# Layer 0's input projection by seven block products in two phases, and its attention by rows

## The chip, the core and the metric

The kernel runs on one core of one Trainium2 chip. The metric is the time of one execution in microseconds (us). Of its engines, TensorE (PE in the profile) multiplies, VectorE (DVE) and ScalarE (ACT) compute on tiles in SBUF and PSUM, GpSimd (POOL) and SyncE (SP) here mainly start DMA transfers. Each engine runs its instructions in order. PSUM has eight banks that each hold one 128 x 512 tile of results.

## The reference

Two decoder layers act on one sequence of 512 tokens of width 2048: layer 0 is gated linear attention (4 heads, keys of 256, values of 512), layer 1 is latent attention. Around each stands a norm before and one after, and the result is added to the input. The change concerns layer 0, whose core is:

```python
def rms_norm(x, g, eps=NORM_EPS):
    xf = x.astype(jnp.float32)
    y = xf * lax.rsqrt(jnp.mean(xf * xf, axis=-1, keepdims=True) + eps)
    return (y * g.astype(jnp.float32)).astype(x.dtype)
...
    proj = h @ w_in
    q, k, v, gate, gk_low = jnp.split(
        proj, [GLA_QK, 2 * GLA_QK, 2 * GLA_QK + GLA_V, 2 * GLA_QK + 2 * GLA_V], axis=-1)
    gk = gk_low @ w_gk2 + b_gk
    log_a = jax.nn.log_sigmoid(gk.astype(jnp.float32)) / GLA_GATE_TAU
...
    b = jnp.cumsum(log_a, axis=3)
...
    q_e = q * jnp.exp(b)
    k_e = k * jnp.exp(-b)
...
    A = jnp.einsum('bhncd,bhnsd->bhncs', q_e, k_e)
...
    o = rms_norm(o, g_onorm).reshape(B, S, GLA_V)
    return (o * jax.nn.silu(gate)) @ w_out
```

The input projection `h @ w_in` has 6144 columns (q, k 1024 each, v and gate 2048 each) and 16 more of the low-rank gate.

## The kernel before

All float32 products with a long moving side are three passes (`mm3`, lines 123 to 127): each operand is split into a high part and the rest, and high*high, high*low and low*high are summed in PSUM. So a 128 x 128 block against 512 columns is three matmuls. The high parts come from ACT, the low ones from DVE, weights included (`chunk_split`, lines 104 to 121), which loads and splits chunks of 1024 elements a partition through rings of buffers.

`start` (line 224) takes x in four tiles of 128 rows. As each is normed, turned by PE transposes (`xn_t`, line 333) and split into `act_hi` and `act_lo`, its products with the first 256 columns of v follow. `gla` (line 339) then does the other v columns of head 0, the low-rank gate product (`gk_low`, line 378, two passes with weights of 48 columns), the decays of head 0 (`decays`, line 419) and for each head the gate and the q and k columns (`block_t`: weights are stationary, the tokens move, so results come transposed), v (`block_s`), the scores (line 488) and the values (line 529). Values come out as o^T, 4 groups of 128 columns; the sum of squares over a head is a product with a matrix of ones (line 549), and the gate is applied in place. `out_proj` (line 558) takes the gated result straight from SBUF.

The norm's gain of layer 0 is multiplied into the weights as they are split (lines 118 and 119). The order of the instructions on each engine is set by a planner that runs the program through a time model and issues what is ready, within the order of the buffers: a tile's buffer comes free when its last reader is done. No due times are written out, apart from two `issue_after` marks for activation tables.

## Time and profile before

| | us |
|---|---|
| median of 3 runs (lowest, highest) | 1508.31 (1508.22, 1508.54) |
| span of the profiled execution | 1506.9 |
| TensorE busy in it | 1488.6 (99%) |
| VectorE busy | 743.9 (49%) |
| ScalarE busy | 659.8 (44%) |
| GpSimd busy | 35.1 (2%) |
| moved by DMA | 149.96 MB, mean 100 GB/s |

Rows of the profile read: line of the code, engine, operation, result<-inputs, tile size and count, then busy time and the mean of one in ns; in the last column the engine's idle time before it and the work that ended it. A row of the timeline starts with the moment and the duration in us. Matmuls overlap, so what one costs is the distance between two starts, and not its own duration. A row of windows gives the length, the busy times of PE, PE's weight loads, DVE, ACT and POOL with their counts, then the granted clock, the DMA share and the GB/s. A row of the chain of waits has start, length, engine, tile and line.

### The profile page before, as it was taken

Reading aid. Unit: us, or ns where it says so; the run is one execution under the profiler, and the core shown is the slowest. Engines: PE = TensorE matmul, PEld = TensorE weight load, DVE = VectorE, ACT = ScalarE, POOL = GpSimd, SP = SyncE. Lnnn points to the kernel's source line nnn. Section 1 sums busy time; section 2 is a strip of 40 time slices with the busy share of each in tenths; the row PEclk is TensorE's granted clock in tenths of the full one; section 3 lists DMA queues with packets and bytes.
Section 4 is the critical chain, followed back from the end, with each engine's and each line's share of the span. In section 5 each row is a group of like instructions: output and inputs, shape, how many; then the busy total and the mean of one; then the engine's idle time right before and its main releaser. Section 6 shows DMA issues by size and latency. Waiting matters only on the chain.

```text
span 1506.9 us, 20016 instructions
## 1 busy us (share of the span) xinstructions
PE 1488.6 (99%) x7874; PEld 1284.5 (85%) x7874; DVE 743.9 (49%) x1345; ACT 659.8 (44%) x1266; POOL 35.1 (2%) x72
## 2 busy tenths in 40 slices
PE   7999999999999999999999999999999999999998
PEld 6988888888888888888899888888888898888888
DVE  6544653355436445434265443333577767753224
ACT  6542642254225424333254444334566676752222
POOL 2100000000000000100011000000000000000000
PEclk9999999999999999999999999999999999999999
DMA  6423223322331323434253333333222112135222
GB/s 222 122 70 98 71 86 96 101 81 80 89 111 57 98 84 120 132 112 133 98 182 100 92 98 98 97 98 91 78 77 66 49 50 72 66 126 182 97 85 112
DMA packets 117966, 149.96 MB, mean 100 GB/s; under 512 B 17580, under 2 KB 75168, under 8 KB 116464
## 3 DMA queue, kind: packets, MB, share of 16 engines
q1 hardware_dynamic: 114272, 136.86, 29.7%
q0 software_dynamic: 3424, 11.75, 2.4%
q8 instruction: 61, 1.00, 0.3%
q14 instruction: 33, 0.27, 0.1%
q10 hardware_dynamic: 176, 0.07, 0.0%
HBM read 140.08 MB, written 8.59 MB: 99 GB/s over the span
## 4 chain that ended last, share of the span: by engine, by line
PE 97%; DMA 1%; DVE 1%; ACT 0%; issue 0%; SPq 0%; DVEq 0%
PE acc L125 11%; PE acc L126 11%; PE acc L127 11%; PE yo_acc L127 8%; PE yo_acc L125 8%; PE yo_acc L126 8%; PE v_acc L127 5%; PE v_acc L126 5%; PE v_acc L125 5%; PE o_t L127 1%; PE o_t L126 1%; PE q_acc L127 1%; PE q_acc L126 1%; PE q_acc L125 1%; PE o_t L125 1%; PE pt L881 1%
## 5 line engine op out<-in xcount | busy, mean ns | idle before, releaser
L125 PE MATMUL acc<-act_hi,w_hi 128*128 128x512 f32 x768 | 299.6, 390 | 0.0
L126 PE MATMUL acc<-act_hi,w_lo 128*128 128x512 f32 x768 | 299.1, 389 | 0.0
L127 PE MATMUL acc<-act_lo,w_hi 128*128 128x512 f32 x768 | 298.8, 391 | 0.0
L119 DVE SCALAR_TENSOR_TENSOR w_lo<-w_raw,g_in,w_hi 128x512 fp32r<-128x512 f32 (+1 forms) x208 | 139.7, 707 | 206.5 <-ACT w_hi L118 206.4
L118 ACT ACTIVATE w_hi<-w_raw,g_in 128x512 fp32r<-128x512 f32 (+1 forms) x200 | 128.2, 691 | 242.7 <-PE acc L127 166.5
L127 PEld LDWEIGHTS acc<-act_lo,w_hi 128*128 128x128 f32 x768 | 144.2, 188 | 30.6 <-issue 0.7
L125 PEld LDWEIGHTS acc<-act_hi,w_hi 128*128 128x128 f32 x768 | 144.2, 188 | 30.6 <-issue 0.7
L126 PEld LDWEIGHTS acc<-act_hi,w_lo 128*128 128x128 f32 x768 | 144.2, 188 | 29.8
L111 DVE TENSOR_TENSOR w_lo<-w_raw,w_hi 128x1024 fp32r<-128x1024 f32 x64 | 78.4, 1225 | 163.6 <-ACT w_hi L110 163.4
L125 PE MATMUL yo_acc<-w_hi,act_hi 128*128 128x512 f32 (+1 forms) x440 | 153.0, 348 | 0.0
L127 PE MATMUL yo_acc<-w_lo,act_hi 128*128 128x512 f32 (+1 forms) x440 | 152.9, 348 | 0.0
L126 PE MATMUL yo_acc<-w_hi,act_lo 128*128 128x512 f32 (+1 forms) x440 | 152.5, 347 | 0.0
L110 ACT CAST w_hi<-w_raw 128x1024 fp32r<-128x1024 f32 x64 | 67.4, 1053 | 163.1 <-PE yo_acc L126 150.0
L119 DVE SCALAR_TENSOR_TENSOR w_lo<-w_raw,gcol,w_hi 128x512 fp32r<-128x512 f32 (+1 forms) x98 | 64.4, 699 | 106.6 <-ACT w_hi L118 106.4
L126 PE MATMUL v_acc<-w_hi,act_lo 128*128 128x512 f32 (+1 forms) x320 | 112.0, 351 | 0.0
L125 PE MATMUL v_acc<-w_hi,act_hi 128*128 128x512 f32 (+1 forms) x320 | 111.3, 351 | 0.4 <-ACT w_hi L118 0.2
L118 ACT ACTIVATE w_hi<-w_raw,gcol 128x512 fp32r<-128x512 f32 (+1 forms) x98 | 61.3, 677 | 114.6 <-PE acc L127 83.8
L127 PE MATMUL v_acc<-w_lo,act_hi 128*128 128x512 f32 (+1 forms) x320 | 110.5, 349 | 0.0
L125 PEld LDWEIGHTS yo_acc<-w_hi,act_hi 128*128 128x128 f32 x440 | 83.4, 189 | 10.4 <-issue 0.2
L126 PEld LDWEIGHTS yo_acc<-w_hi,act_lo 128*128 128x128 f32 x440 | 83.3, 189 | 10.3
L127 PEld LDWEIGHTS yo_acc<-w_lo,act_hi 128*128 128x128 f32 x440 | 83.2, 189 | 10.4 <-issue 0.2
L126 PE MATMUL yo_acc<-w_hi,y_lo 128*128 128x512 f32 (+1 forms) x200 | 69.5, 348 | 0.0
(300 smaller groups left out, 2724.3 us busy)
## 6 DMA issues: line engine op xcount, KB each, us to landing
w_raw<-in_l_gla_w_in_dram SPq DMA_DIRECT2D x64, 512.0 KB, 3.7
w_raw<-in_l_mla_w_in_dram SPq DMA_DIRECT2D x47, 512.0 KB, 3.7
w_raw<-in_l_gla_w_in_dram SPq DMA_DIRECT2D x64, 256.0 KB, 3.0
w_raw<-in_l_gla_w_out_dram SPq DMA_DIRECT2D x32, 512.0 KB, 3.5
w_raw<-in_l_mla_w_out_dram SPq DMA_DIRECT2D x32, 512.0 KB, 3.5
pw_raw<-in_l_mla_w_kvb_dram SPq DMA_DIRECT2D x64, 128.0 KB, 2.5
xo<-in_x_dram POOLq DMA_DIRECT2D x16, 256.0 KB, 5.7
x1d<-yo SPq DMA_DIRECT2D x4, 1024.0 KB, 6.0
```

Source lines behind the costliest of these rows:

```text
L110: nc.scalar.copy(hi, raw)
L111: nc.vector.tensor_tensor(lo, raw, hi.bitcast(F32), ALU.subtract)
L118: nc.scalar.activation(hi[:, kk, :], raw[:, kk, :], AF.Copy, scale=g)
L119: nc.vector.scalar_tensor_tensor(lo[:, kk, :], raw[:, kk, :], g, hi[:, kk, :].bitcast(F32), ALU.mult, ALU.subtract)
L125: t.matmul(out, lh, rh, start=start, stop=False)
L126: t.matmul(out, ll, rh, start=False, stop=False)
L127: t.matmul(out, lh, rl, start=False, stop=stop)
L881: te.transpose(pt[:, o:o + P], probs[i][:, j * P:(j + 1) * P], self.ident)
```

## The change

The 12 blocks of 512 columns of layer 0's input projection become six pairs: q with k (`qk(0)`, `qk(1)`: two heads each) and v with gate (`vg(0)` to `vg(3)`). For each pair, two halves of the tokens, pairs of row blocks of the weights and the two column blocks form 2 x 2 x 2 blocks, which the Strassen-Winograd form multiplies with seven block products and sums instead of eight. Activations (and sums of them) are now the stationary side throughout; the weights (and sums of them), 512 wide, move.

There are two phases over all six pairs. In the first, `first_four` (line 253 of the changed code) does four of the seven products for each pair into eight PSUM banks `pa0` to `pa7`: for each of the eight pairs of row blocks it loads 512 KB twice, makes three sums on DVE and splits. It writes the partial results `p1` and `vw` to DRAM (`stage`) through POOL's queue. Then `left_rest` (line 374) rebuilds the activation sums in the places they had, and in the second phase `last_three` (line 286) does the other three products into `pb0` to `pb5`, reads the partial results back and forms the four results `c0` to `c3`. For q and k, `qk_evac` (line 579) transposes them in PSUM (`qk_t`), two banks alternating. The decays are made for two heads at once, in 2048-wide operations (line 538), one result for q and one for k.

`start` (line 320) now norms all four row tiles and keeps the turned result in float32 (`ht`), and `left_sums` (line 362) makes sums of the token halves before the first product. The low-rank gate product (`gk_low`, line 498) is 16 matmuls in plain float32 from `ht`, goes to DRAM and is read back by `gk_spread` (line 510) after `left_rest`, since it takes `ht`'s memory. The values (line 657) come by rows of tokens; the norm of a head is per row and ACT's accumulated squares replace the ones product; its gain moves into the output weights. Gated rows go to DRAM (`yd`), and `gla_rows` (line 674) reads them back, transposes and splits them ahead of the output projection.

```diff
@@ build
             self.ln_exp_set()
-            self.start()
             self.gla()
...
+            self.gla_rows()
             self.out_proj(a["l0_gla_w_out"], a["l0_post_norm"],
-                                lambda k: (self.act_hi[:, k, :], self.act_lo[:, k, :]),
-                                self.between, self.cq_ahead)
+                          lambda k: (self.act_hi[:, k, :], self.act_lo[:, k, :]),
+                          self.between, self.cq_ahead, gain=self.gon16)
...
+    def act_slot(self, t, kp, slot, r):
+
+        o = (slot % 2) * 256 + r * P
+        return t[:, 2 * kp + slot // 2, o:o + P]
...
+    def prods(self, ps, kp, slots, hi, lo, ws):
+        for q, (slot, wi) in enumerate(zip(slots, ws)):
+            for r in range(2):
+                self.mm3(ps[2 * q + r], self.act_slot(self.act_hi, kp, slot, r),
+                         self.act_slot(self.act_lo, kp, slot, r), hi[:, wi, :], lo[:, wi, :],
+                         kp == 0, kp == KT // 2 - 1)
+
+    def first_four(self, w, m, n1, n2):
...
+        ps = [self.ps.tile([P, 512], F32, tag="a", name=f"pa{q}", bufs=8) for q in range(8)]
+        for kp in range(KT // 2):
+            r1 = self.raw_pair(w, n1, kp, name="left")
+            r2 = self.raw_pair(w, n2, kp, name="right")
...
+            v.tensor_tensor(t[:, 0, :], r1[:, 0, :], r2[:, 0, :], ALU.add)
+            v.tensor_tensor(t[:, 1, :], t[:, 0, :], r2[:, 1, :], ALU.add)
+            v.tensor_tensor(t[:, 2, :], t[:, 1, :], r1[:, 1, :], ALU.add)
...
+            nc.scalar.copy(hi[:, 1:4, :], t)
+            v.tensor_tensor(lo[:, 1:4, :], t, hi[:, 1:4, :].bitcast(F32), ALU.subtract)
+            self.prods(ps, kp, (0, 2, 1, 3), hi, lo, (0, 2, 1, 3))
+        for r in range(2):
+            p1 = self.stg([P, 512], "p1")
+            nc.scalar.copy(p1, ps[r])
+            nc.gpsimd.dma_start(self.stage[m, :, 0, r, :], p1)
+            u = self.stg([P, 512], "u2")
+            v.tensor_tensor(u, p1, ps[2 + r], ALU.subtract)
+            for i, p in ((1, ps[4 + r]), (2, ps[6 + r])):
+                t = self.stg([P, 512], "vw")
+                v.tensor_tensor(t, u, p, ALU.add)
+                nc.gpsimd.dma_start(self.stage[m, :, i, r, :], t)
...
+    def last_three(self, w, m, n1, n2, evac):
...
+        ps = [self.ps.tile([P, 512], F32, tag="b", name=f"pb{q}", bufs=6) for q in range(6)]
+        done = self.sp.tile([P, 3, 2, 512], F32, tag="done", name="done", bufs=1)
+        nc.gpsimd.dma_start(done, self.stage[m])
+        for kp in range(KT // 2):
...
+            v.tensor_tensor(t, r2[:, 0, :], r2[:, 1, :], ALU.add)
...
+            self.prods(ps, kp, (2, 0, 1), hi, lo, (0, 1, 2))
+        for r in range(2):
+            p2, q3, p7 = ps[r], ps[2 + r], ps[4 + r]
+            c = [self.stg([P, 512], f"c{i}") for i in range(4)]
+            v.tensor_tensor(c[0], p2, done[:, 0, r, :], ALU.add)
+            evac(r, 0, c[0])
...
@@ start
-                self.part_s(s, 4 * i, ws[i], self.v_ps, slice(0, 256), self.act_hi, self.act_lo, KT)
...
+                    v.scalar_tensor_tensor(xt[s][:, c], xt[s][:, c], rstd, gr[:, c], ALU.mult, ALU.mult)
...
+                    nc.scalar.copy(self.ht[:, 4 * g:4 * g + 4, cols], pv)
+                    ks = slice(4 * g + s // 2, 4 * g + 4, 2)
+                    self.split_from(pv[:, s // 2::2, :], self.act_hi[:, ks, cols], self.act_lo[:, ks, cols])
             for g in range(4):
...
+                self.left_sums(xp, g)
...
+    def left_rest(self, g):
...
+        v.tensor_tensor(x[:, :, 0, :], h(1, 1), h(0, 1), ALU.subtract)
+        v.tensor_tensor(x[:, :, 0, :], x[:, :, 0, :], h(0, 0), ALU.add)
+        v.tensor_tensor(x[:, :, 0, :], h(1, 0), x[:, :, 0, :], ALU.subtract)
+        v.tensor_tensor(x[:, :, 1, :], h(0, 0), h(0, 1), ALU.subtract)
...
@@ gla
+        order = [qk(0), vg(0), vg(1), qk(1), vg(2), vg(3)]
...
+                    self.constants()
+                    self.gk_low()
+                    for m, (n1, n2) in enumerate(order):
+                        self.first_four(w, m, n1, n2)
+            with pool("lb", **R) as self.tp:
+                for g in range(4):
+                    self.left_rest(g)
...
+            self.gk_spread()
+            with tc.issue_after(self.ln_exp.ins):
+                self.decays(0)
+            for p in range(2):
+                self.last_three(w, 3 * p, *qk(p), self.qk_evac)
+                for h in (2 * p, 2 * p + 1):
+                    self.scores(h)
+                    self.last_three(w, 3 * p + 1 + h % 2, *vg(h), self.vg_begin(h))
+                    self.values(h)
+                if p == 0:
+                    self.decays(1)
...
@@ gk_low
-            nc.tensor.matmul(ps[0:m, :], wl[:, k, :], self.act_hi[:, k, :], start=k == 0, stop=False)
-            nc.tensor.matmul(ps[0:m, :], wl[:, k, :], self.act_lo[:, k, :], start=False, stop=k == KT - 1)
...
+            nc.tensor.matmul(ps[0:GRANK, :], raw[:, k, :], self.ht[:, k, :], start=k == 0, stop=k == KT - 1)
...
@@ decays, qk_evac
+        nc.scalar.activation(ek, ek, AF.Exp, scale=-1.0)
+        nc.scalar.activation(ek, ek, AF.Ln, bias=1.0)
+        v.tensor_tensor(ek, eq, ek, ALU.subtract)
...
+        pt = self.pt("qk_t")
+        for j in range(4):
+            nc.tensor.transpose(pt[:, j * P:(j + 1) * P], c[:, j * P:(j + 1) * P], self.ident)
...
@@ values, gla_rows
+                self.mm3(po, at(self.at_h, j)[:, c], at(self.at_l, j)[:, c], self.vh[j], self.vl[j],
+                         j == 0, j == i)
...
+            v.scalar_tensor_tensor(y, po, r, y, ALU.mult, ALU.mult)
+            nc.gpsimd.dma_start(self.yd[h, :, i, :], y)
+
+    def gla_rows(self):
...
+            y = self.slot(f"g{h}", [P, ST, GDV], F32, f"y{h}")
+            nc.sync.dma_start(y, self.yd[h])
...
```

Three places in the order of the instructions, before and changed. The first is the start on PE. Before, `v_acc0` are products of v and `xn_t` transposes of normed x:

```order
L333 MATMUL xn_t_125<-cf_87,xn_123 128x128 x4
L333 MATMUL xn_t_134<-cf_87,xn_132 128x128 x4
L125 MATMUL v_acc0_109<-w_hi_159,act_hi_78 128x256
L333 MATMUL xn_t_143<-cf_87,xn_141 128x128 x4
L126 MATMUL v_acc0_109<-w_hi_159,act_lo_79 128x256
L127 MATMUL v_acc0_109<-w_lo_160,act_hi_78 128x256
L125 MATMUL v_acc0_109<-w_hi_159,act_hi_78 128x256
L126 MATMUL v_acc0_109<-w_hi_159,act_lo_79 128x256
```

Now, with `gkl_acc` the low-rank gate product, `gkl_raw` its weights, `ht` the turned x and `pa0` the first product of the new form:

```order
L353 MATMUL xn_t_270<-cf_82,x3_101 128x128 x4
L353 MATMUL xn_t_279<-cf_82,x3_101 128x128 x4
L411 MATMUL gcols_331<-cf_82,rows_323 128x36
L504 MATMUL gkl_acc_367<-ht_75,gkl_raw_365 16x512 x16
L130 MATMUL pa0_388<-w_hi_404,act_hi_66 128x512
L131 MATMUL pa0_388<-w_hi_404,act_lo_67 128x512
L132 MATMUL pa0_388<-w_lo_405,act_hi_66 128x512
```

The products that stood between transposes are gone, and the low-rank gate product stands ahead of the first product of the projection. Its weights come from POOL, whose row waits for the last split of the sums (`act_lo<-lsum_297`) on DVE:

```order
L406 DMA rows_323<-in_l1_pre_norm_dram 16x128
L501 DMA gkl_raw_365<-in_l0_gla_w_in_dram 128x16x16
L445 DMA trigd_361<-sin_cos_353 128x128 x2
L445 DMA trigd_361<-nsn_359 128x128
L508 DMA gkd_386<-gkl_384 16x512
```

On DVE the sums of the token halves (`lsum`) and their splits stand so:

```order
L368 TENSOR_TENSOR lsum_292<-lsum_292,ht_75 128x2x256
L372 TENSOR_TENSOR act_lo_67<-lsum_287,act_hi_66 128x2x512
L372 TENSOR_TENSOR act_lo_67<-lsum_292,act_hi_66 128x2x512
L367 TENSOR_TENSOR lsum_297<-ht_75 128x2x256
L367 TENSOR_TENSOR lsum_302<-ht_75 128x2x256
L368 TENSOR_TENSOR lsum_297<-lsum_297,ht_75 128x2x256
L368 TENSOR_TENSOR lsum_302<-lsum_302,ht_75 128x2x256
L372 TENSOR_TENSOR act_lo_67<-lsum_297,act_hi_66 128x2x512
```

On POOL the load of the weights stands behind the small rows of constants; on DVE four splits and their sums stand behind those of the last row tile.

The second place is the change from the first q/k pair to the first v/gate pair in the second phase, on PE (`pb` are products, `c0` to `c3` results, `qk_t` their transposes):

```order
L132 MATMUL pb2_2902<-w_lo_2947,act_hi_66 128x512
L584 MATMUL qk_t_2788<-cf_82,c0_2783 128x128 x4
L584 MATMUL qk_t_2795<-cf_82,c1_2784 128x128 x4
...
L132 MATMUL pb4_2904<-w_lo_2947,act_hi_66 128x512
L584 MATMUL qk_t_2802<-cf_82,c2_2785 128x128 x4
L584 MATMUL qk_t_2809<-cf_82,c3_2786 128x128 x4
L584 MATMUL qk_t_2820<-cf_82,c0_2815 128x128 x4
L584 MATMUL qk_t_2827<-cf_82,c1_2816 128x128 x4
L130 MATMUL pb5_2905<-w_hi_2914,act_hi_66 128x512
```

and on DVE, where `eq` and `ek` are the decays of two heads:

```order
L551 TENSOR_SCALAR eq_2479<-z_2493,gcol_333 128x512
...
L307 TENSOR_TENSOR c0_2815<-pb1_2520,done_2525 128x512
L309 TENSOR_TENSOR c1_2816<-pb3_2522,done_2525 128x512
L554 TENSOR_TENSOR ek_2480<-eq_2479,ek_2480 128x2048
L556 SCALAR_TENSOR_TENSOR eq_2479<-restart_2476,ek_2480 128x512 x4
L563 TENSOR_TENSOR rest_2505<-eq_2479 128x12
L573 TENSOR_TENSOR ek_2480<-eq_2479 128x2048
...
L588 SCALAR_TENSOR_TENSOR eq_2479<-qk_t_2788,eq_2479 128x4x128
L588 SCALAR_TENSOR_TENSOR eq_2479<-qk_t_2802,eq_2479 128x4x128
L311 TENSOR_TENSOR c2_2817<-pb5_2524,done_2525 128x512
```

Where PE's rows are left out stand 11 products more; `qk_t_2802` takes the bank of `qk_t_2788`, whose reader is the row after the subtraction, the scans and the second subtraction on DVE.

The third place is the entry to the output projection, on SP (`w_raw` are output weights, `y0` to `y3` the gated rows) and on PE (`o_` values, `y_t` transposes):

```order
L103 DMA w_raw_5212<-in_l0_gla_w_out_dram 128x2x512
L103 DMA w_raw_5244<-in_l0_gla_w_out_dram 128x2x512
L103 DMA w_raw_5276<-in_l0_gla_w_out_dram 128x2x512
L679 DMA y0_4944<-yd_69 128x2048
L679 DMA y1_4974<-yd_69 128x2048
L679 DMA y2_5004<-yd_69 128x2048
L679 DMA y3_5034<-yd_69 128x2048
L103 DMA w_raw_5312<-in_l0_gla_w_out_dram 128x2x512
```

On PE:

```order
L130 MATMUL o_4903<-v_hi3_4543,at_h2_4502 128x512
L131 MATMUL o_4903<-v_hi3_4543,at_l2_4505 128x512
L132 MATMUL o_4903<-v_lo3_4547,at_h2_4502 128x512
L683 MATMUL y_t_4946<-cf_82,y0_4944 128x128 x4
L683 MATMUL y_t_4953<-cf_82,y0_4944 128x128 x4
L130 MATMUL yo_acc0_5080<-w_hi_5086,act_hi_66 128x512
```

The load of the gated rows stands behind seven loads of weights, the last of which (`w_raw_5276`) takes a buffer that DVE's split of the fourth (`w_lo_5183`) frees. Before, no such load existed, and products of the output projection stood between those of the last values:

```order
L127 MATMUL yo_acc1_4733<-w_lo_4829,act_hi_78 128x512
L125 MATMUL yo_acc1_4733<-w_hi_4828,act_hi_78 128x512
L126 MATMUL yo_acc1_4733<-w_hi_4828,act_lo_79 128x512
L549 MATMUL o_norm_4675<-o_ssq_4608,ones_547 128x512
L127 MATMUL yo_acc1_4733<-w_lo_4829,act_hi_78 128x512
L125 MATMUL yo_acc2_4734<-w_hi_4828,act_hi_78 128x512
```

More of the change, by code (lines that the diff above doesn't have):

```diff
@@ L44 @@
 SCALE = (NOPE + ROPE) ** -0.5
+NMAC = 6
 GQ0, GK0, GV0, GG0, GL0 = 0, 1024, 2048, 4096, 6144
@@ new lines, in left_sums @@
+    def left_sums(self, pool, g):
+        nc, v = self.nc, self.nc.vector
+        h = lambda odd, half: self.ht[:, 4 * g + odd:4 * g + 4:2, half * 256:(half + 1) * 256]
+        x = pool.tile([P, 2, 2, 256], F32, tag="lsum", name="lsum", bufs=2)
+        v.tensor_tensor(x[:, :, 0, :], h(1, 1), h(0, 1), ALU.subtract)
+        v.tensor_tensor(x[:, :, 1, :], x[:, :, 0, :], h(0, 0), ALU.add)
+        sl = lambda t: (t[:, 4 * g:4 * g + 4, :].rearrange("p (q k) n -> p q (k n)", k=2)[:, :, 256:768]
+                        .rearrange("p q (s n) -> p q s n", s=2))
+        nc.scalar.copy(sl(self.act_hi), x)
+        v.tensor_tensor(sl(self.act_lo), x, sl(self.act_hi).bitcast(F32), ALU.subtract)
@@ L339, in gla @@
     def gla(self):
[L340 removed]
+        nc, tc, a = self.nc, self.tc, self.a
         w = a["l0_gla_w_in"]
[L342 to L363 removed]
@@ L398, in gk_low @@
-        both = self.slot("g3", [96, 1024 + S], FR, "gk2_r")
+        both = self.gp.tile([96, 1024 + S], FR, name="gk2_r")
         self.w2, self.g2 = both[:, 0:1024], both[:, 1024:]
-        for i, t in enumerate(w2):
+        for i in range(2):
+            t = self.tmp([96, 512], F32, f"w2{i}")
             c = slice(i * 512, (i + 1) * 512)
@@ L423, in decays @@
         nc, v = self.nc, self.nc.vector
[L424 to L431 removed]
+        eq = self.bp.tile([P, 4, S], F32, tag="eq", name="eq")
@@ new lines, in decays @@
+            v.tensor_scalar(eq[:, c, :], z, bias, 0.0, ALU.add, ALU.min)
+        nc.scalar.activation(ek, ek, AF.Exp, scale=-1.0)
+        nc.scalar.activation(ek, ek, AF.Ln, bias=1.0)
+        v.tensor_tensor(ek, eq, ek, ALU.subtract)
+        for c in range(4):
+            v.tensor_tensor_scan(eq[:, c, :], self.restart, ek[:, c, :], 0.0, ALU.mult, ALU.add)
+        b = eq.rearrange("p c (j t) -> p (c j) t", t=P)
+        mid = eq.rearrange("p c (j t) -> p c j t", t=P)[:, :, :, GCH - 1]
+        end = eq.rearrange("p c (j t) -> p c j t", t=P)[:, :, :, P - 1]
@@ new lines, in decays @@
+        f = self.st.tile([P, 4, 6], F32, tag="far", name="far", bufs=2)
+        r = self.st.tile([P, 4, 3], F32, tag="rest", name="rest", bufs=2)
+        v.tensor_tensor(r, end[:, :, 0:3], mid[:, :, 0:3], ALU.subtract)
+        for o, i in ((0, 0), (3, 1), (5, 2)):
+            v.tensor_tensor(f[:, :, o:o + 1], r[:, :, i:i + 1], mid[:, :, i + 1:i + 2], ALU.add)
+        v.tensor_tensor(r[:, :, 0:2], r[:, :, 0:2], end[:, :, 1:3], ALU.add)
+        for o, i in ((1, 0), (4, 1)):
+            v.tensor_tensor(f[:, :, o:o + 1], r[:, :, i:i + 1], mid[:, :, i + 2:i + 3], ALU.add)
@@ new lines, in gla_rows @@
+    def gla_rows(self):
+        nc = self.nc
+        for h in range(GH):
+            y = self.slot(f"g{h}", [P, ST, GDV], F32, f"y{h}")
+            nc.sync.dma_start(y, self.yd[h])
+            for s in range(ST):
+                pt = self.pst.tile([P, 512], F32, tag="pt", name="y_t")
+                for j in range(4):
+                    nc.tensor.transpose(pt[:, j * P:(j + 1) * P], y[:, s, j * P:(j + 1) * P], self.ident)
+                cols = slice(s * P, (s + 1) * P)
+                self.split_from(pt.rearrange("p (k n) -> p k n", n=P),
+                                self.act_hi[:, 4 * h:4 * h + 4, cols], self.act_lo[:, 4 * h:4 * h + 4, cols])
@@ L559, in out_proj @@
+    def out_proj(self, w, gpost, y_of, then, ahead=None, gain=None):
         nc, v = self.nc, self.nc.vector
```

363 lines of the change are left out of this document (176 added, 187 removed).

## The prediction

> **What bounds the kernel now.** I read the engine rows of the page first, then the chain of waits, then the spacing of TensorE's instructions.
>
> ```profile
> span 1506.9 us, 20016 instructions
> PE 1488.6 (99%) x7874; PEld 1284.5 (85%) x7874; DVE 743.9 (49%) x1345; ACT 659.8 (44%) x1266; POOL 35.1 (2%) x72
> PE 97%; DMA 1%; DVE 1%; ACT 0%; issue 0%; SPq 0%; DVEq 0%
> ```
>
> TensorE (PE) works without a pause, and the chain that ends last is 97% PE. So the time is the sum of the products' spacings plus the few pauses, and a product that disappears is worth its whole spacing, as long as PE does not wait for what takes its place. The spacing, from the timeline of PE:
>
> ```profile
> 199.66 0.39 PE L127 MATMUL acc<-act_lo,w_hi 128*128 128x512 f32 x1
> 199.88 0.39 PE L125 MATMUL acc<-act_hi,w_hi 128*128 128x512 f32 x1
> ...
> 202.15 0.40 PE L126 MATMUL acc<-act_hi,w_lo 128*128 128x512 f32 x1
> ```
>
> Eleven intervals lie between the first and the last row: (202.15 - 199.66)/11 = 0.2264 us for one 512-wide product. Where layer 0 now hands over to its output projection, and how the first 70 us go:
>
> ```profile
> 599.36 0.58 PE L125 MATMUL yo_acc<-w_hi,act_hi 128*128 128x512 f32 x1
> 0.00:27.00 27.00, 15.96 (x98) 14.54 (x99) 16.99 (x46) 20.44 (x55) 5.24 (x17) 1.00 0.84 283
> 27.00:70.00 43.00, 43.00 (x358) 42.47 (x357) 27.72 (x67) 22.58 (x43) 8.38 (x15) 1.00 0.39 111
> ```
>
> The second and third rows are windows (PE is the first busy time): PE works 16 of the first 27 us and then without a gap, because products of v start on each row tile as it arrives. At 599.4 the first output product starts, with the last score tiles (about 1.3 us), 48 value products of the last head (about 7.5) and one ones product (0.9) still behind it: PE has done all work before the output projection at an equivalent of **609 us**. What follows is alike in both programs: 576 output products of 512 columns, 384 of 256, then layer 1. The gain of the inner norm that moves into the weights' split there (two half-width instructions an engine instead of one) hides under PE's 24 products (5.4 us) a pair of rows. So I forecast only the moment that replaces 609.
>
> **The products.** Before, the six column pairs of the input projection are 12 column blocks x 4 token tiles x 16 rows of blocks x 3 passes = 2304 products; now 6 x 8 x 24 in the first phase and 6 x 8 x 18 in the second, 2016. That is 521.7 us against 456.4: **-65.2 us**. Small work on PE, from these rows:
>
> ```profile
> 202.54 0.86 PE o_norm L549 x2
> 164.27 1.78 PE a_diag L506 x16
> 166.06 1.31 PE a_off L524 x8
> 171.95 1.34 PE a_off L524 x12
> 22.77 0.66 PE L333 MATMUL xn_t<-cf,xn 128*128 128x128 f32 x4 [0.16 <-DVE act_lo L175]
> 23.18 0.36 PE L126 MATMUL v_acc<-w_hi,act_lo 128*128 128x256 f32 x1
> ```
>
> Scores stay 4.43 a head, 17.7 in all. Four 128-wide transposes take 0.41 (22.77 to the next start); 64 new ones for q and k and 64 for the gated rows are 2 x 16 x 0.41 = 13.1. Values by rows are 30 products a head, 4 x 30 x 0.2264 = 27.2; eight z products 1.9. The ones product in plain fp32 (two records) takes 0.86 for 512 columns.
>
> **The start** eats most of the gain. All products of the new form need sums of two row tiles, so none can start until all four tiles are normed, turned and summed. And ahead of them on PE now stands the low-rank gate product, 16 instructions in plain fp32: by the 0.86 row, 13.8 us. It waits for its weights, whose DMA on POOL waits for the last split of the sums (DVE's row act_lo<-lsum, because the memory is only then free).
>
> ```profile
> L330 DVE TENSOR_SCALAR xn<-x,x_rstd x16: 476/482/487, 9.2 to 31.8; 128x512 f32<-128x512 f32 x16
> L111 DVE TENSOR_TENSOR w_lo<-w_raw,w_hi 128x1024 fp32r<-128x1024 f32 x4 | 4.9, 1226 | 5.0 <-ACT w_hi L110 5.0
> L464 DVE SCALAR_TENSOR_TENSOR eqm<-acc,eqm 128x512 f32<-128x512 f32 x8 | 5.5, 684 | 0.0
> L175 DVE TENSOR_TENSOR at_l<-a_off,at_h 128x256 fp32r<-128x256 f32 x3 | 1.3, 425 | 11.9 <-ACT at_h L174 11.9
> gkl_raw<-in_l_gla_w_in_dram POOLq DMA_DIRECT2D x1, 128.0 KB, 4.0
> ```
>
> DVE up to that split, at these durations: 16 norm instructions with two tensors (0.69 each, 11.0), 16 splits of 256 (6.8), 12 weight sums that stand between them (8.3), two weight splits of 512 and two of 1536 (1.4 and, by the slope of 0.54 per 512 from the 512 and 1024 rows, 3.5), 8 sums of act (5.5) and 4 splits of 1024 (4.9): 41 us. DVE began at 9.2 before, so the split ends near 50, or 53 with some waits for ACT. Plus 4.0 for the weights' DMA and 13.8: the first product starts at **71 us** (bounds 64, if DVE keeps the closer pitch of about 0.6 that back-to-back rows show, and 76). Without any stall behind it the handover is at 71 + 456.4 + 13.1 + 1.9 + 17.7 + 27.2 = **587 us**, 22 before today's 609. The change can therefore afford 22 us of stalls.
>
> **The stalls**, each as order of instructions times durations:
>
> ```profile
> L442 DVE TENSOR_TENSOR_SCAN b<-restart,soft 128x512 f32<-128x512 f32 x8 | 9.8, 1222 | 0.2
> L110 ACT CAST w_hi<-w_raw 128x1024 fp32r<-128x1024 f32 x4 | 4.2, 1048 | 4.3 <-PE v_acc L126 4.3
> L438 ACT ACTIVATE soft<-soft 128x512 f32<-128x512 f32 x8 | 5.0, 631 | 0.2
> x1d<-yo SPq DMA_DIRECT2D x4, 1024.0 KB, 6.0
> w_raw<-in_l_gla_w_in_dram SPq DMA_DIRECT2D x64, 512.0 KB, 3.7
> act_hi<-x1d POOLq DMA_DIRECT2D x2, 1024.0 KB, 7.3
> trigd<-sin_cos POOLq DMA_DIRECT2D x2, 64.0 KB, 2.5
> ```
>
> A 2048-wide operation is not in the trace: bounds are the 1024 row and four times the 512 row, and by the slopes I take 2.3 on DVE and 1.9 on ACT.
>
> *Decays.* Late in each q/k column pair PE has given its last z product; then run two ACT operations of 512 (1.3), exp and ln of 2048 (3.8), a DVE subtraction (2.3), four scans (4.9), a second subtraction (2.3), small pieces (1.0) and exp of 2048 (1.9): 17.5 us until DVE empties the first transposed q tile. Two banks hold such tiles, so the third q/k transpose waits for that, and everything of PE stands behind it. In between PE has only 27 products and 8 transposes (6.9): 10.6 idle, and about 1.4 more at the next pair of tiles, 12. In the second q/k pair some 34 products lie between: 10. Together **22** (15 to 30). If the order let PE run on into the next pair's products, this would be nothing; the banks of the next pair are emptied by the same DVE queue.
>
> *Between phases.* After the last product of the first phase, PE can do the 12 products whose act slots stay (2.7), then needs slots rebuilt by DVE sums whose memory is freed when the last partial result has left for DRAM: two DVE results, its DMA on POOL (2.5 to 5), four sums, a cast of 1024, about 13.4 after the last product. Idle **11** (8 to 14).
>
> *Changes of column pair.* PE overtakes the emptying of its banks by one or two DVE results: 1.5 each by the 0.69 row with its cast, five times in the first phase and three in the second: **12** (0 to 20).
>
> *The end.* The gated rows are read back from DRAM. That load stands on SP behind seven loads of output weights, of which the last waits for DVE's split of the fourth; about 26 DVE instructions (16 us) lie between the last product of the input projection and that split, and the load of 1 MB takes 6.0 to 7.3, then transposes and splits 1.2. PE has the 30 value products (6.8) to fill 23.7: idle **16** (10 to 20). If the load stood first it would be covered by nothing but those value products.
>
> Within a phase PE is not overtaken: a pair of row blocks is 24 products, 5.4 us, against 4.5 on DVE (three sums of 0.69, splits of 0.69 and 1.77) and about 2.1 on ACT; in the second phase 4.1 against 2.8 and 1.9. Loads are 1 MB a 5.4 us, two of the 3.7 us rows, on queues whose window row shows 283 GB/s where 193 are needed.
>
> *Clock.* PE pauses longer than any in today's steady part, and its start shows what a cold start does:
>
> ```profile
> 15.75 0.41 PE L125 MATMUL v_acc<-w_hi,act_hi 128*128 128x256 f32 x1
> 15.96 0.41 PE L126 MATMUL v_acc<-w_hi,act_lo 128*128 128x256 f32 x1
> ...
> 18.06 0.28 PE L127 MATMUL v_acc<-w_lo,act_hi 128*128 128x256 f32 x1
> 18.18 0.28 PE L125 MATMUL v_acc<-w_hi,act_hi 128*128 128x256 f32 x1
> ```
>
> The same product is 0.21 apart at 15.8 and 0.12 apart at 18.1, after some 4 us of dense work; the granted clock in the window row reads 1.00 all the same. Four stalls of 9 us or more would each cost 0 to 1.7 us by these rows; I take 3 for all. [...]
>
> **Sum.** 587 + 22 + 11 + 12 + 16 + 3 = 651 against 609: +42. The profiled span of 1506.9 becomes 1549; the median of the runs lies 1.4 above that span, so **1550 us**.
>
> **The rivals.** (A) *Faster, 1497.* The planner's order is better than my walk: scans and sums overlap, DVE keeps 0.6 throughout. With the start at 64, decays 2, phases 5, changes 0 and the end 6, the handover is 580 + 13 = 593, 16 early: 1492; with half of the spared stalls back, 1497. For it: the arithmetic is sure to save 65, and DVE is busy only 49%. Against it: the four waits are on PE in program order, whatever the load. (B) *Some stalls smaller, still slower: 1522.* All at their lower bounds (15, 8, 0, 10) with the start at 71: 587 + 33 = 620, +11, or 1519; 1515 to 1530 when one of them is full. (C) *Slower by much: 1585.* One mechanism, DVE in the first phase: my 4.5 us of a 5.4 pair become 5.9 if DVE runs 30% slower beside the loads; 48 pairs x 0.5 = 24 more, then cold clocks add 4 to 10. For it: three sums and a 1536 split of each pair are new work; against it: the rows of today give DVE one duration from 27 to 70 us, where it is busy 64% of the window (27.72 of 43), and later. (D) *It does not do what it says:* products stay 0.2264 but the stalls eat exactly the gain, 1506 to 1511: it needs 22 us of stalls, less than half of what I walk.
>
> **Chances.** Forecast (1533 to 1570) 0.55; B (1513 to 1533) 0.15; C 0.14; A 0.12; D 0.04. What can be told from no change is about 0.2%, 3 us. The likeliest case's range is 1533 to 1570; for 8 in 10 it reaches down through B and up into C: 1512 to 1582. Faster 0.12, same 0.04, slower 0.84.
>
> **What would show it.** PE busy about 50 to 60 us less, with 95% of the span; first 512-wide product near 71 us behind 16 fp32 products; PE idle of 10 us at two qk_t rows, each released by DVE, with an exp of 2048 in front; idle of about 11 before pb2 of the first second-phase pair; idle of about 16 before y_t, released by a DMA. If the first product starts before 62 us, or if the sum of idle time on PE from there to the output projection is under 22, the forecast is wrong by its sign; if DVE is 90% busy in the first phase, C is it.

## The result, and the profile after

| | before | changed |
|---|---|---|
| median of 4 runs, us | 1508.42 | 1565.57 |
| lowest, highest | 1508.22, 1509.31 | 1561.76, 1567.71 |
| profiled span, us | 1506.9 | 1564.0 |

The ratio is 1.0374 (95%: 1.0359 to 1.0388): the changed kernel is 57 us slower. The forecast was 1550 with a range of 1512 to 1582.

From the page of the changed kernel: the span, the engine rows, the granted clock in 40 slices, and the shares of the chain that ended last.

```profile
span 1564.0 us, 19919 instructions
PE 1463.3 (94%) x7409; PEld 1234.4 (79%) x7409; DVE 978.1 (63%) x1652; ACT 729.7 (47%) x1391; POOL 68.6 (4%) x130
PEclk7799999999899989799999999999999999999999
PE 70%; issue 18%; DVE 6%; DMA 3%; ACT 2%; POOL 1%; SPq 0%; DVEq 0%; POOLq 0%; ACTq 0%
```

PE has 465 instructions fewer. It is busy 25 us less, and the span is 57 us longer. The granted clock, which gave 1.00 over the window from 27 to 70 us before, now falls below nine tenths in five of the slices (slices of 39 us; the first two, the eleventh, the fifteenth and the seventeenth).

Where PE waits, by the work that ended the wait (us in total, times, longest):

```profile
PE xn_t L353 <- DVE x L350: 27.4, 4, 13.0
PE qk_t L584 <- DVE eq L588: 23.2, 4, 11.0
PE gkl_acc L504 <- DMA gkl_raw<-in_l_gla_w_in_dram: 9.5, 1, 9.5
PE pb L130 <- ACT act_hi L384: 7.6, 1, 7.6
PE gcols L411 <- DMA rows<-in_l_pre_norm_dram: 5.2, 1, 5.2
PE o L130 <- DVE sg L671: 4.7, 2, 2.6
PE y_t L683 <- DMA y<-yd: 4.3, 1, 4.3
```

These are the places that the prediction had walked: the start without products (`xn_t` and `gcols`; PE's waits at its start sum to 11 us in the kernel before), the decays, the low-rank gate product, the change of phase, the last values and the reload of the gated rows. The first product of the new form starts here (timeline of PE):

```profile
71.30 1.45 PE L504 MATMUL gkl_acc<-ht,gkl_raw 128*16 128x512 f32 x3
72.68 0.50 PE L130 MATMUL pa<-w_hi,act_hi 128*128 128x512 f32 x1
```

And this is the program by stage (windows: length, busy time of PE, of its weight loads, of DVE, ACT and POOL, then granted clock, DMA share, GB/s): the first phase, the two stalls of the decays, and the end of layer 0's attention.

```profile
72.70:337.00 264.30, 262.88 (x1153) 214.97 (x1152) 215.32 (x261) 101.04 (x108) 17.57 (x33) 1.00 0.68 207
...
398.00:420.00 22.00, 10.50 (x45) 8.52 (x45) 17.46 (x30) 7.16 (x9) 0.55 (x1) 0.69 0.24 85
...
538.00:560.00 22.00, 10.12 (x47) 7.97 (x46) 17.56 (x29) 7.16 (x9) 0.54 (x1) 0.69 0.19 68
...
631.00:656.00 25.00, 12.46 (x33) 8.09 (x31) 17.38 (x29) 16.79 (x39) 3.76 (x7) 0.70 0.57 196
```

The first phase runs as costed: 1152 products at 0.2264 us are 260.8, and it took 264.3. Each stall takes two things. In the 22 us around the decays PE is busy 10.5, and the mean clock of that stretch is 0.69: the work after the stall runs slow too. The first of the two, on PE:

```profile
397.66 0.39 PE L132 MATMUL pb<-w_lo,act_hi 128*128 128x512 f32 x1
408.68 1.09 PE L584 MATMUL qk_t<-cf,c 128*128 128x128 f32 x4 [10.63 <-DVE eq L588]
...
414.37 0.63 PE L132 MATMUL pb<-w_lo,act_hi 128*128 128x512 f32 x1
414.79 0.63 PE L130 MATMUL pb<-w_hi,act_hi 128*128 128x512 f32 x1
```

PE waits 10.63 us for DVE's `eq`, and 6 us after it resumed its products still stand 0.42 apart instead of 0.2264.

### The profile page after: what moved, and what is told of

It is laid out like the page before. It is cut to its first block, busy times and chain, and to the rows that moved or that the text cites. A ratio compares the mean times of both kernels' runs of the same rounds, so it can differ in the third digit from the quotient of the medians.

```text
span 1564.0 us, 19919 instructions
## 1 busy us (share of the span) xinstructions
PE 1463.3 (94%) x7409; PEld 1234.4 (79%) x7409; DVE 978.1 (63%) x1652; ACT 729.7 (47%) x1391; POOL 68.6 (4%) x130
## 4 chain that ended last, share of the span: by engine, by line
PE 70%; issue 18%; DVE 6%; DMA 3%; ACT 2%; POOL 1%; SPq 0%; DVEq 0%; POOLq 0%; ACTq 0%
PE yo_acc L130 8%; PE yo_acc L132 8%; PE yo_acc L131 8%; PE pb L130 4%; PE pb L131 4%; PE pb L132 3%; PE acc L132 3%; PE acc L131 3%; PE acc L130 3%; PE q_acc L132 1%; PE q_acc L131 1%; PE q_acc L130 1%; PE pt L1012 1%; DMA right<-in_l_gla_w_in_dram 1%; PE cq_acc L131 1%
## 5 line engine op out<-in xcount | busy, mean ns | idle before, releaser
L130 PE MATMUL pa<-w_hi,act_hi 128*128 128x512 f32 x384 | 150.4, 392 | 1.4 <-ACT p L274 1.4
L131 PE MATMUL pa<-w_hi,act_lo 128*128 128x512 f32 x384 | 149.5, 389 | 0.0
L130 PE MATMUL pb<-w_hi,act_hi 128*128 128x512 f32 x288 | 116.4, 408 | 12.7 <-ACT act_hi L384 7.6
L132 PE MATMUL pa<-w_lo,act_hi 128*128 128x512 f32 x384 | 118.3, 389 | 0.0
L131 PE MATMUL pb<-w_hi,act_lo 128*128 128x512 f32 x288 | 114.0, 397 | 0.0
L132 PE MATMUL pb<-w_lo,act_hi 128*128 128x512 f32 x288 | 101.0, 398 | 0.8 <-DVE w_lo L302 0.8
L130 PE MATMUL acc<-act_hi,w_hi 128*128 128x512 f32 x256 | 99.7, 389 | 0.0
L131 PE MATMUL acc<-act_hi,w_lo 128*128 128x512 f32 x256 | 99.6, 389 | 0.0
L132 PE MATMUL acc<-act_lo,w_hi 128*128 128x512 f32 x256 | 99.1, 389 | 0.0
L270 DVE TENSOR_TENSOR w_lo<-sums,w_hi 128x1536 fp32r<-128x1536 f32 x48 | 84.2, 1754 | 15.1 <-ACT w_hi L269 15.1
L130 PEld LDWEIGHTS yo_acc<-w_hi,act_hi 128*128 128x128 f32 x440 | 83.7, 190 | 10.5 <-ACT act_hi L179 0.2
```

The lines of the kernel that those rows point to most:

```text
L130: t.matmul(out, lh, rh, start=start, stop=False)
L131: t.matmul(out, ll, rh, start=False, stop=False)
L132: t.matmul(out, lh, rl, start=False, stop=stop)
L270: v.tensor_tensor(lo[:, 1:4, :], t, hi[:, 1:4, :].bitcast(F32), ALU.subtract)
```

## The experiments

The first theory was the prediction's: each stall lies in the order of the instructions, and taking away what makes PE wait gives back the stall. Its rival: a stall that goes comes back a little later as a wait for VectorE, which is busy 63% of the span now. A second question came with the profile: whether the half clock behind a stall is part of the stall's price. All ratios are against the kernel before (1508.44 to 1508.49 in these runs).

**The weights of the low-rank gate early.** They are loaded at the start into a buffer that is there anyway, so that the load waits for no memory.

```diff
@@ start
+        raw = self.wp.tile([P, 2, 512], F32, tag="left2", name="gkl_raw", bufs=3)
+        self.gkl_raw = raw[:, 0, 0:KT * GRANK].rearrange("p (k n) -> p k n", n=GRANK)
+        nc.gpsimd.dma_start(self.gkl_raw, ...)
@@ gk_low
-        raw = self.tp.tile([P, KT, GRANK], F32, tag="gkl_raw", name="gkl_raw")
-        nc.gpsimd.dma_start(raw, ...)
+        raw = self.gkl_raw
```

> One edit: the weights of the low-rank gate product are loaded at the start into a buffer of the weight ring, so that their load no longer waits for the last split of the token-half sums. Theory (the start is a chain: last split, load 4 us, 13.8 us of float32 products in front of the first new product): TensorE's idle of 9.5 us in front of the float32 products goes to under 1 us, the first new product starts at about 63 us instead of 72.7, and the median falls by 9 to 10 us, to about 1556 us. Rival (the start is bound by VectorE, which makes rows, sums and splits): the idle moves from in front of the float32 products to in front of the first new product, which still starts after 70 us, and the median stays at 1562 to 1568 us.

1557.96 us, 1.0334 (1.0318 to 1.035): 7.6 less than the change. The gate product starts at 48.65 instead of 56.8, the first new product at 64.0 instead of 72.68. The wait of 9.5 us for the weights was real, and most of it comes back.

**The gate product behind the first phase.** The other way to have it off the start:

```diff
@@ gla
-                    self.gk_low()
                     for m, (n1, n2) in enumerate(order):
                         self.first_four(w, m, n1, n2)
+                    self.gk_low()
```

> One edit: the low-rank gate product moves from in front of the first phase to behind it, into the place where TensorE waits for the rebuilt activation sums. Theory (at the start the product and the wait for its weights are 18 us of delay; behind the first phase it fills a wait of 11.7 us that is there anyway, and the half clock after that wait comes from its idle time): the first new product starts at 54 to 56 us instead of 72.7, TensorE's idle between the phases falls to 1 to 4 us, no half-clock stretch stands between 320 and 345 us, and the median is 1545 to 1550 us. Rival one (the start is bound by VectorE, which still has weights to split): first new product after 62 us, 1555 us or more. Rival two (the half clock comes from load): the half-clock stretches at the change of phase stay, 1551 to 1556 us.

1549.47, 1.0276 (1.026 to 1.0291): 16.1 less. The first new product starts at 47.3. The gate product now fills the change of phase. Its row in this kernel, and the window of that change here and, in the second fence, in the changed kernel:

```profile
L504 PE MATMUL gkl_acc<-ht,gkl_raw x32: 592/592/603, 320.7 to 334.0; 128*16 128x512 f32 x32
310.00:345.00 35.00, 35.00 (x126) 20.16 (x125) 26.38 (x39) 12.78 (x20) 3.75 (x7) 1.00 0.48 159
```

```profile
310.00:345.00 35.00, 30.90 (x129) 24.57 (x128) 26.16 (x36) 13.53 (x18) 3.23 (x6) 0.94 0.49 158
```

With PE busy through the change of phase the clock stays at 1.00, where it fell in the changed kernel with the same work on the other engines. So here the half clock went with PE's idle time (1.00 against 0.94 in this window). The start gains less than the 25 us by which its first product is earlier: after 21 products PE waits 4.45 us for `gcol`, a copy that stands in DVE's queue behind its work on masks and angles (53.4 to 58.1), and the gate product's own 14 us are only moved.

**The v/gate products ahead of the q/k products.** In each half of the second phase the v/gate products of the first head go ahead of the q/k products, so that PE has 144 products to run while the decays are made.

```diff
@@ gla
             for p in range(2):
+                h = 2 * p
+                self.last_three(w, 3 * p + 1, *vg(h), self.vg_begin(h))
                 self.last_three(w, 3 * p, *qk(p), self.qk_evac)
-                for h in (2 * p, 2 * p + 1):
-                    self.scores(h)
-                    self.last_three(w, 3 * p + 1 + h % 2, *vg(h), self.vg_begin(h))
-                    self.values(h)
+                self.scores(h)
+                self.values(h)
+                self.scores(h + 1)
                 if p == 0:
                     self.decays(1)
+                self.last_three(w, 3 * p + 2, *vg(h + 1), self.vg_begin(h + 1))
+                self.values(h + 1)
```

> One edit: in the second phase the first v/gate pair of each two heads comes before their q/k pair, and the decays of the second two heads are made before the last but one v/gate pair, so that the 17 us chain of exp, ln, scans and exp has a whole pair (about 33 us of products) beside it. Theory (TensorE waits for that chain at the third q/k transpose, and the half clock of 13.65 us after each such stall is set by the idle time itself): both idle stretches of 11 us at qk_t go, with them the half-clock stretches at 402 and 542 us, and the median falls by 23.2 + 6.0 = 29 us, to about 1536 us (1533 to 1542). Rival one (the half clock comes from load, not from idle time): the idle goes but a half-clock stretch stays somewhere between 390 and 560 us, 1540 to 1546 us. Rival two (VectorE is the bound of this part, it is busy 86% from 380 to 420 us): the idle reappears in front of scores or values and the median stays above 1555 us.

1551.70, 1.0288 (1.0271 to 1.0306): 13.9 less, half of what was expected. The waits of PE in this kernel:

```profile
PE o L130 <- DVE at_l L180: 8.6, 2, 7.2
PE pb L130 <- DVE c L307: 7.8, 4, 4.5
...
PE pb L132 <- DVE w_lo L302: 4.6, 3, 3.4
...
PE qk_t L587 <- DVE c L307: 0.4, 1, 0.4
```

The wait of `qk_t` went from 23.2 to 0.4. The first three rows are 21.0 us of waits for DVE. Of these the changed kernel had 1.3 too, and the 8.6 at `at_l` stand at the last values, where it waited 8.3 for other operands. So some 11 us are new, at the results and splits of the next products; the longest split wait, 3.4 us, stands right behind the four scans on DVE. Here the rival holds for half the gain: the decays still occupy DVE, and PE now meets its queue at the next results and splits.

**The decays with less work on ScalarE.** The exp and ln of 2048 columns, 3.8 us of the chain as the prediction had it, are left out, so the decays are not those of the reference.

```diff
@@ decays
-        nc.scalar.activation(ek, ek, AF.Exp, scale=-1.0)
-        nc.scalar.activation(ek, ek, AF.Ln, bias=1.0)
```

> Left out: the exp and the ln of 2048 columns in the decays (two ScalarE instructions of 1.9 us for each two heads), so that the chain between the last z product and the release of the first transposed q tile is 3.8 us shorter. Theory (the stall is that chain less the products beside it): the idle in front of the third q/k transpose falls from 10.6 and 11.0 us to 6.8 and 7.2, and the median falls by 7.6 us of idle and up to 4 us of half clock, to 1554 to 1559 us. Rival (VectorE's queue sets it, whatever ScalarE does): idle stays above 9 us each, 1562 us or more.

1566.28, 1.0385 (1.0369 to 1.04): no gain. DVE's timeline ahead of the stall, first in the changed kernel:

```profile
395.50 2.28 DVE L554 TENSOR_TENSOR ek<-eq,ek 128x2048 f32<-128x2048 f32 x1
397.81 4.57 DVE L556 TENSOR_TENSOR_SCAN eq<-restart,ek 128x512 f32<-128x512 f32 x4
...
402.51 2.28 DVE L573 TENSOR_TENSOR ek<-eq 128x2048 f32<-128x2048 f32 x1
...
407.85 0.69 DVE L588 SCALAR_TENSOR_TENSOR eq<-qk_t,eq 128x512 f32<-128x512 f32 x1 [2.09 <-ACT eq L575]
```

and ScalarE's there:

```profile
390.29 1.92 ACT L552 ACTIVATE ek<-ek 128x2048 f32<-128x2048 f32 x1
392.25 1.91 ACT L553 ACTIVATE ek<-ek 128x2048 f32<-128x2048 f32 x1
405.79 0.22 ACT L571 ACTIVATE far<-far 128x24 f32<-128x24 f32 x1 [11.63 <-DVE far L570]
405.92 1.89 ACT L575 ACTIVATE eq<-ek 128x2048 f32<-128x2048 f32 x1
```

then DVE's without exp and ln:

```profile
394.83 2.28 DVE L552 TENSOR_TENSOR ek<-eq,ek 128x2048 f32<-128x2048 f32 x1
...
397.62 4.56 DVE L554 TENSOR_TENSOR_SCAN eq<-restart,ek 128x512 f32<-128x512 f32 x4
...
407.65 0.69 DVE L586 SCALAR_TENSOR_TENSOR eq<-qk_t,eq 128x512 f32<-128x512 f32 x1 [2.09 <-ACT eq L573]
```

ln ended at 394.16, and the subtraction that takes its result started 1.3 us later, because DVE was in results, sums and splits of the products without a pause. So 3.8 us of ScalarE were worth 0.2 at the end (407.85 to 407.65). The idle time at `qk_t` fell by 2.9 in all (23.2 to 20.3), in part because PE came later to it: it waited 1.15 and 0.56 for results of DVE just ahead. And two other stretches of half clock, those that end the change of phase and the values, came out 3.4 longer each, and the half clock costs 2.8 more in this execution, added up over every product in such a stretch. That leaves no gain, as the rival had it.

**The decays with less work on DVE.** The same question from the other side: the four scans are left out, so the running sums within a chunk are missing.

```diff
@@ decays
-        for c in range(4):
-            v.tensor_tensor_scan(eq[:, c, :], self.restart, ek[:, c, :], 0.0, ALU.mult, ALU.add)
```

> Left out: the four scans (running sums of the log decays) for each two heads, 4.57 us of VectorE in a row. ScalarE's exp and ln of the decays stay. Theory, corrected by the run with shorter decays (there VectorE worked without a pause from 387 to 405.8 us, so its queue and not ScalarE's exp and ln is the chain): the idle in front of the third q/k transpose falls by the whole 4.6 us, from 10.6 and 11.0 to 6.0 and 6.4 us. The median falls by 9 us of idle and up to 7 us more if the half clock gets shorter with it, 1549 to 1557 us. Rival (some other chain of the same length stands beside it, ScalarE or the loads): less than 2 us each, above 1560 us.

1556.47, 1.0318 (1.0301 to 1.0335): 9.1 less. PE's wait (23.2 in the changed kernel), the kernel without exp and ln first, then that without scans:

```profile
PE qk_t L582 <- DVE eq L586: 20.3, 4, 9.7
```

```profile
PE qk_t L582 <- DVE eq L586: 13.0, 4, 5.7
```

Each stall is 5 us shorter than in the changed kernel for 4.57 us of scans. The two runs together put the chain in DVE's queue as far as the second subtraction, and not in the operations in the order in which the data pass through them; behind it DVE does wait, 2.09 us, for ScalarE's exp. No run took out a DVE instruction that stands in this queue and is no part of the decays.

**The gated rows through POOL's queue.** If SP's weight loads ahead hold up the reload, another queue should not.

```diff
@@ gla_rows
-            nc.sync.dma_start(y, self.yd[h])
+            nc.gpsimd.dma_start(y, self.yd[h])
```

> One edit: the gated rows are read back through GpSimd's queue instead of SyncE's, where they stood behind seven loads of output weights. Theory (that place on the queue sets the last wait): TensorE's idle of 4.3 us in front of the first transposes goes, and with it part of the half clock there; the median falls by 4 to 7 us, to 1559 to 1562 us. Rival (the wait is that of the values and the gate on VectorE, and the load would be hidden anyway): the idle grows in front of the value products or stays, 1563 to 1568 us.

1571.05, 1.0408 (1.0392 to 1.0424): 5.5 more. **The rows ahead of the weights.** Here SP's loads of output weights wait until the first load of gated rows is issued, and the rows of the last head, whose writing ends last, go through POOL's queue, so that they hold up nothing on SP.

```diff
+            with tc.issue_after(self.y_load.ins):
                 self.out_proj(...)
@@ gla_rows
-            nc.sync.dma_start(y, self.yd[h])
+            ld = (nc.gpsimd if h == GH - 1 else nc.sync).dma_start(y, self.yd[h])
+            if h == 0:
+                self.y_load = ld
```

> One edit: on SyncE's queue the loads of the gated rows of heads 0 to 2 stand ahead of the loads of output weights instead of behind seven of them; the rows of head 3 are loaded by GpSimd's queue behind their last write. Theory (the place on the queue keeps the load of the first rows 15 us behind the last projection product): the load starts near 631 us instead of 646, TensorE's idle of 4.3 us in front of the first transposes goes and half a stretch of half clock with it, median 1558 to 1562 us; the value products keep their own waits of 8 us. Rival (output weights are late in their turn, since they now wait behind the rows): an idle of 3 us or more in front of the first output products, 1563 to 1570 us.

1559.69, 1.034 (1.0325 to 1.0356): 5.9 less. The issues of these loads (count, duration in ns, first and last start), in the changed kernel, through POOL, and ahead of the weights:

```profile
L679 SPq DMA_DIRECT2D y<-yd x4: 320/340/618, 646.2 to 661.2; - x4
```

```profile
L679 POOL DMA_DIRECT2D y<-yd x4: 527/532/538, 651.5 to 654.1; - x4
```

```profile
L680 SPq DMA_DIRECT2D y<-yd x3: 320/339/342, 632.6 to 633.6; - x3
```

On POOL the first load stood behind the last write of gated rows and came 5.3 us later; PE's wait grew from 4.29 to 8.74. So the first edit did not test what it was to test. In the second the load starts 13.6 us earlier, and `y_t` no longer waits for a DMA. But this edit also moves the loads of output weights, and with them their splits. PE's waits in it:

```profile
PE y_t L686 <- DVE act_lo L180: 3.7, 6, 1.8
PE o L130 <- DVE sg L672: 0.8, 1, 0.8
```

The transposes wait 3.7 us for DVE where they waited 4.3 for the load, and the values wait 0.8 for `sg` instead of 4.7: in the changed kernel DVE had eight splits of output weights among the gates between 637.4 and 645.6 us, and here none before 656.2. So what stood ahead of the load in its queue decided when it started here (646.2, 651.5 and 632.6 us), as the prediction had it; how much of the 5.9 us came from that, and how much from the later splits, is not separated.

**The edits together.** The first three (weights early, v/gate first, rows through POOL):

> The three edits together: the weights of the low-rank product early, v/gate before q/k, the rows by GpSimd's queue. Theory (three separate places on one chain of TensorE): the gains add, 9.5 + 29 + 5 = 43 us, to about 1522 us (1517 to 1528), still slower than the kernel before by about 14 us, since 63 us of start and some 20 us of smaller stalls remain. Rival (the places share one limit, VectorE): less than 30 us together, above 1535 us.

1552.77, 1.0298 (1.028 to 1.0316). Singly they give -7.6, -13.9 and +5.5, which would make 1549.6: they add up to within 3.2 us. So the 1522 was missed by its terms, and not by the adding. And the better form of each (gate product late, v/gate first, rows first):

> Three edits together: the low-rank gate product behind the first phase, v/gate before q/k in the second, gated rows ahead of the output weights. From the single runs: 18 us at the start, 14 us as measured for v/gate first, 4 us at the end. Theory (separate waits of TensorE on its one line of work): 1526 to 1534 us, slower than the kernel before still, by 18 to 26 us, because the start without products (54 us against 16 us of idle today) and the 144 extra transposes stay. Rival (VectorE is the common limit, 79% busy over the second phase): above 1538 us.

1533.19, 1.0169 (1.0152 to 1.0186): 32.4 less, where the single edits sum to 35.9. It is the best version found, and 25 us slower than the kernel before. What PE still waits for in it:

```profile
PE pb L130 <- DVE c L308: 8.7, 4, 4.5
PE pb L130 <- ACT w_hi L302: 6.7, 2, 4.2
PE o L130 <- DVE at_l L180: 5.9, 2, 4.4
```

Between 340 and 660 us it has 26.8 us of idle time and 9.1 of half clock. Without these 36 it would take some 1497, an estimate from those two sums: the saved products are there. The start still stands against them, with 33 us of waits ahead of the first new product where the kernel before had 11. That the waits of the second phase come from the work that the form adds on DVE is argued from these rows, and not shown by a run.

**The sums of the second phase on GpSimd.** One way to unload DVE in that version, 48 additions of 128 x 512:

```diff
@@ last_three
-            v.tensor_tensor(t, r2[:, 0, :], r2[:, 1, :], ALU.add)
+            nc.gpsimd.tensor_tensor(t, r2[:, 0, :], r2[:, 1, :], ALU.add)
```

> On top of the three edits together: the 48 weight sums of the second phase run on GpSimd instead of VectorE, 29 us of VectorE's queue at a pitch of 0.6 us. Theory (what is left of idle time in the second phase, 26.8 us with 9 us of half clock, is VectorE's queue at the changes of pair): the idle of TensorE between 340 and 660 us falls below 20 us and the median falls by 5 to 12 us, to 1521 to 1528 us. [...] Rival two (the waits are dependences, not the queue): 1530 to 1536 us.

1539.95, 1.0208 (1.0192 to 1.0223): 6.8 more than without this edit. The groups (busy, mean ns): DVE's first split of a pair in the version without it, then that split and GpSimd's sum with it.

```profile
L303 DVE TENSOR_TENSOR w_lo<-left,w_hi 128x512 fp32r<-128x512 f32 x48 | 32.9, 686 | 5.8 <-ACT w_hi L302 3.9 <-ACT ek L556 1.5
```

```profile
L303 DVE TENSOR_TENSOR w_lo<-left,w_hi 128x512 fp32r<-128x512 f32 x48 | 40.2, 838 | 19.0 <-ACT w_hi L302 18.4 <-issue 0.4
```

```profile
L298 POOL TENSOR_TENSOR sum<-right 128x512 f32<-128x512 f32 x48 | 80.1, 1670 | 123.1 <-DVE w_lo L303 85.2 <-DMA right<-in_l_gla_w_in_dram 32.5 <-DVE rest L570 1.9
```

GpSimd needs 1.67 us where DVE needed 0.69, DVE sits idle for 19.0 us before this split instead of 5.8, and the split itself is 22% longer. Of the 33 us of sums that DVE is spared, the three splits of a pair take back 13.7 (98.5 us before, 112.2 now). DVE's busy time between 340 and 660 us fell only from 258.5 to 255.0, so this run does not show what a less busy DVE would be worth.

## Why the prediction was right, and by which steps

The sign and the size were right: 1550 forecast, 1565.6 measured, inside the likeliest case's own range of 1533 to 1570, and the large stalls stand at the places named. That the sum is as near as this is in part luck: two terms were 11.9 too high (changes of column pair, last values and reload) and took back most of the 14.9 by which the clock was too low. One of the prediction's signs missed: PE was to be busy 50 to 60 us less, and is 25 less, mostly because the same work took longer at half clock and by the 5.3 us below. The terms, each against its own row. Half clock was added up over every product that started in a stretch of half clock, as its spacing beyond the usual one.

| term | forecast, us | measured, us |
|---|---|---|
| first new product | 71 | 72.7 |
| work of PE from there to the reload | 509.7 | 511.8, and 5.3 not accounted for |
| decays | 22 | 23.2 |
| between phases | 11 | 11.7 |
| changes of column pair | 12 | 3.6 |
| last values and reload | 16 | 12.5 |
| half clock | 3 | 15.1, and 2.8 behind the reload |

Summed to the first `y_t` the measured terms give 656.0. With 6.6 for these transposes and the last 2.8 the handover is at 665.4; it was forecast at 651 and stood at 609 before. What follows took 897.9 before and 898.6 now, as assumed.

- *The start* held. The gate product waited for its weights behind a split of the sums, as walked, though it was the last but one that released the load, at 52.3 (forecast 50 to 53). The product itself took 15.8 us instead of 13.8: PE was at half clock until 60.9, which the half-clock row above does not count. Behind the first phase, at full clock, it took 13.8. Moving the load or the product gave 7.6 and 16.1 us.
- *The products* held to 0.4%. The 5.3 us of longer spacings without a wait or a lower clock stay open.
- *The decays* held in size and failed in their chain. "17.5 us until DVE empties the first transposed q tile" counted ScalarE's exp and ln; they are hidden (3.8 us of them gave 0.2), and DVE's results, sums and splits stand in their place ahead of the subtraction. Without the scans, which are in that queue, 4.57 us gave about 5 at each stall. The right number came from a sum with one wrong and one missing part.
- *Between phases* held, and the late gate product covers it whole.
- *Changes of column pair* failed: forecast 12, measured 3.6. PE did not overtake the emptying of its banks by one or two DVE results each time; the longest such wait is 1.22, the two in the first phase that show in the trace 0.7 each.
- *The end* was oversized. The load was issued 15.3 us after the last product of the projection (630.9 to 646.2), as walked, and the first `y_t` started 9.8 us later, where 6.0 to 7.3 had been taken for the load. But the values in front of it had waits of their own (1.91, 1.68, 2.09 and 2.57 for ScalarE's and DVE's splits and gates), so only 4.3 us of the load were left to wait for: 12.5 in all, where 16 had been put on the load alone.
- *The clock* is the step that failed most: "I take 3 for all", measured 17.9. The price from the start of before (0 to 1.7 for each of four stalls) came from a single transition. Here the half clock costs 4.3 at the change of phase (two stretches), 3.4 and 2.6 at the decays and 4.8 at the last values. PE is at half clock for 3.2 to 7.2 us after a stall (it resumed at 354.7, 408.7 and 550.2, full clock at 357.9, 415.9 and 555.8), and the clock fell around shorter waits too: ahead of the change of phase (at 340.8, PE busy 0.73 of the 3.4 us before) and within the last values (at 637.8, busy 1.24 of 3.4). The sum was too small because there were six stretches instead of four, and each of the four places cost 2.6 to 4.8, where 1.7 had been the most.

Of the rivals, A (faster) asked for stalls of 2, 5, 0 and 6, and the runs show 23, 12, 4 and 12. B asked for all of them at their lower bounds; the changes of pair and the end came towards theirs, the other two did not, and the clock took back what was spared. C put DVE behind in the first phase: it is busy 215 of 264 us there and PE is not held up. The 4 to 10 us that C adds for cold clocks are shown by no run; the half clock measured, 17.9, came behind other waits. D needs 22 us of stalls; there are 51 and 18 of half clock.

## What to carry to other kernels

On a kernel whose bound engine never pauses, price a saved product at its full spacing, but first walk the queue of the engine that has to make the new operands: at the decays here, what stood ahead of the awaited instructions in that queue set the stall more than the chain of data did. Price each stall of TensorE with half clock on top (2.6 to 4.8 us by place in the changed kernel), a group of short waits too, and look for independent products to put there; a stall that is covered so can come back as waits at the same busy engine (some 11 of 23 us did here). The reload from DRAM waited here for what stood ahead of it in its own queue, so choose the queue by its last instruction before the load (the start moved from 646.2 to 651.5 on POOL, and to 632.6 ahead of the weights).

## What the runs showed of the hardware

Between 330 and 700 us of the changed kernel's trace the granted clock stands at half in six stretches: 340.8 to 347.6, 351.0 to 357.9, 402.2 to 415.9, 542.2 to 555.8, 637.8 to 651.4 and 654.8 to 661.7 us. Three lasted 6.8 us and three 13.65, and in this trace the twelve moments lie whole multiples of 3.41 us apart (the 201.4 us from 340.8 to 542.2 are 59 of them). Four windows around the first decays:

```profile
398.80:402.20 3.40, 0.00 (x0) 0.00 (x0) 3.40 (x4) 0.00 (x0) 0.00 (x0) 1.00 0.00 0
402.20:405.60 3.40, 0.00 (x0) 0.00 (x0) 3.30 (x11) 0.00 (x0) 0.00 (x0) 0.51 0.00 0
...
409.00:412.50 3.50, 2.64 (x12) 1.84 (x11) 2.68 (x5) 0.76 (x1) 0.00 (x0) 0.50 0.00 0
412.50:415.90 3.40, 3.40 (x12) 2.89 (x11) 2.43 (x5) 1.30 (x3) 0.55 (x1) 0.50 0.44 101
```

In the 3.4 us ahead of 402.2 PE had no work, and behind them the clock was at half. In the window in which PE is busy 2.64 of 3.5 us it reads 0.50, in the full one behind it 0.50 still, and from 415.9 on 1.00. Ahead of the other five stretches PE was busy 0.73 (ahead of 340.8), 0.00 (351.0), 0.38 (542.2), 1.24 (637.8) and 0.30 us (654.8) of 3.4. So PE was not idle throughout ahead of each fall. In the last 3.4 us of the six stretches it was busy 2.93 to 3.40. How long a wait must be to lower the clock, or how much work brings it back, no run was made to show.

In the kernel before, the window from 0 to 27 us reads 1.00, though the products of 256 columns stand 0.21 apart at 15.8 and 0.12 at 18.1: that reading does not tell how fast PE ran there.

The changed kernel's four runs spread over 0.4% (1561.76 to 1567.71 us), those of before over 0.07% (1508.22 to 1509.31). Of the four the fastest had the highest mean clock (0.972, the others 0.967 to 0.970); the cause was not tested further.
